# Memory tokens turned unscaled, two heads' key-query products ahead, and another order of the score products

## The chip, the cores and the metric

The kernel runs on one core of a Trainium2 chip. The metric is the device time of one execution in microseconds. TensorE (PE) multiplies matrices into PSUM, which has eight banks of 128 x 512 float32. VectorE (DVE) and ScalarE (ACT) work on data in SBUF and PSUM, and SyncE (SP) issues all the DMAs.

## The reference, cut to what matters

One decoder layer on x of 2048 x 1024, in float32, with 256 memory tokens: a recurrent and convolutional mixer, cross-attention into the memory, a gated feed-forward network and a last norm. The attention is the part that the change touches:

```python
h = rms_norm(x, xa_norm_g[l])
m = rms_norm(mem, mem_norm_g[l])                    # 256 x 1024
q = (h @ w_q[l]).reshape(bsz, s, XA_HEADS, XA_HD)   # 4 heads of 256
kv = m @ w_kv[l]
k, v = jnp.split(kv, 2, axis=-1)
...
scores = jnp.einsum("bshd,bmhd->bhsm", q, k).astype(jnp.float32) * (XA_HD ** -0.5)
p = jax.nn.softmax(scores, axis=-1).astype(v.dtype)
o = jnp.einsum("bhsm,bmhd->bshd", p, v).reshape(bsz, s, d)
x = x + o @ w_o[l]
```

Here rms_norm divides each token by the root of its mean square (plus 1e-6) and multiplies with a gain per channel.

## The kernel before

The kernel does not issue its instructions as it goes. Its Python code records operations (`Program.do`, `Program.dma`; all are issued from line 485), and a planner then simulates the engines at build time (`Program.schedule`, `Program.deadlines`) and writes out one fixed order for each engine. The order of the recorded matmuls gives each operation a due time; on each engine the ready operation with the earliest due time goes first. The durations that the planner assumes come from `estimate`. Operations recorded while `pr.first` is true come before all others. 28 passes are simulated, and the order of the shortest is written out. So a change of an assumed duration moves no work, but can move instructions within each engine's order, SP's DMAs included.

All large matmuls are done as three products of operands split into a high and a low part (`mm3`, names ending in h and l). ScalarE writes the high part and VectorE the low part.

The stages, in order of time:
- `memory_a` (start): the 256 memory tokens are loaded as four 128 x 512 tiles `mem`, squared and summed, scaled with their norm factor, transposed by TensorE with the identity, and copied with the channel gain to four tiles `mt` (channels x tokens). For each head, `kv` multiplies `mt` with columns of w_kv (`raw`) to give the keys, the columns of w_q are transposed (`qt`), and their product gives A, that is w_q times the keys: x times A is the scores. `HEADS` heads are done ahead of the first half's mixer, the other heads behind it (`mixed_in`).
- `mix_x`, `mix`: the tokens x are normed and transposed, and multiplied with w_in, in two halves of 1024 tokens. VectorE does the convolutions (`conv`) and the recurrence (`lru`, with one scan for each of 16 tiles), the second half's while the first half is in its attention.
- `attend(0)`, `attend(1)`: for each half of the tokens three matrix products (w_out, A, and VO, which is values times w_o), each done by `seven` as Strassen's scheme with seven block products P1 to P7. A product is 4 steps of inner blocks x 4 token blocks x 3 matmuls. It accumulates in a group of four PSUM banks, a or b; all eight are then taken. A product either starts a group afresh (True) or adds to what the group holds (False). When a product ends, the group is read into the blocks C11 to C22 that its row names; the next product on that group has to wait for these drains.
- For the second of the three (`SECOND`, the scores), the drains go to tiles `prob`: the first into a block is a copy by ScalarE, the later ones are additions by VectorE, and behind the last one the tile's softmax runs: maximum on VectorE, two exponentials with sums on ScalarE, a reciprocal, two scalings on ScalarE. Then `turn` transposes the block on TensorE to tiles `pt`, which the third product (`THIRD`) reads. The table given to `seven` says behind which product and which inner step a turn or a norm is recorded: (6, 0) is behind step 0 of the seventh product.
- `up`, `Down`, `finish`: the feed-forward network and the last norm, from about 1035 us to the end.

Of the kernel before, what the change touches and what calls it, by code (L numbers as in the profile page):

```python
# [62 lines left out]
STACKS = 2  # L63


def estimate(eng, name, n, pointer):
    if eng == "DVE":
        if name == "reciprocal":
            return 0.1 + n * 0.0063
        return (0.13 if name == "scalar_tensor_tensor" else 0.08) + n * 0.00104  # L70
    if eng == "Pool":
        return 0.18 + n * 0.0021
    return 0.1 + n * 0.00083 + 0.09 * pointer


class Buf:
# [90 lines left out]
class Program:  # L167
# [51 lines left out]
    def do(self, eng, name, out, *args, reads=(), writes=(), **kw):  # L219
        outs = [out] + ([kw["accum_out"]] if "accum_out" in kw else [])  # L220
        ins = [a for a in list(args) + list(kw.values()) if isinstance(a, Ref) and a not in outs]
        if eng == "PE":
            o = self.group or self.op("PE")
            n = ins[1].n if name == "matmul" else P
            if name == "matmul":
                cost = (n + 32) / 2400.0 if ins[1].rounded else n * 4 / 2400.0
            else:
                cost = 0.11
            self.clock += cost
            o.cost += cost  # L230
        else:
            o = self.op("Pool" if eng == "either" else eng)
            o.either = eng == "either"
            n = max(r.n for r in ins + outs)
            o.cost = estimate(o.eng, name, n, any(isinstance(a, Ref) for a in kw.values()))
            if eng == "DVE":
                self.vector = max(self.vector, self.clock) + o.cost
            if eng == "ACT":
                o.sets = ACT_SETS.get(args[1])
        o.calls.append((name, (out,) + args, kw))  # L240
        for r in outs:
            if not r.rounded:
                r.buf.loaded = False
        self.touch(
            o, [b for r in ins for b in r.parts()] + [b.parts[0] for b in reads],
            [b for r in outs for b in r.parts()] + [b.parts[0] for b in writes],
        )
# [72 lines left out]
    def schedule(self):  # L320
# [81 lines left out]
        def dispatch(e, t):  # L402
            if not idle[e]:
                return
            o = pick(e, t)
            if o is None:
                return
            idle[e] = False
            o.start, o.on = t, e
            order.append(o)  # L410
            if e == "PE":
                lag[0] += 0.2 * (t - o.turn - lag[0])
            cost = o.cost
            if e == "ACT" and o.sets is not None and table[0] not in o.sets:
                cost += ACT_SWITCH
                table[0] = o.sets[0]
            if o.either and e == "DVE":
                cost = estimate("DVE", "tensor_tensor", 1024, False)
            if e == "SP":
                dma_free[0] = max(dma_free[0], t) + cost  # L420
                push(max(t + 0.1, dma_free[0] - BACKLOG), 2, e)
                push(dma_free[0] + o.delay, 0, o)
            else:
                push(t + cost, 2, e)
                push(t + cost, 0, o)
# [87 lines left out]
def hybrid_layer(  # L513
# [25 lines left out]
    def ACT(out, in_, func, **k):  # L539
        pr.do("ACT", "activation", out, in_, func, **k)  # L540
# [14 lines left out]
    def ps():  # L555
        return pr.new("ps", name="ps")
# [57 lines left out]
    def small(w):  # L614
        at, n_small[0] = n_small[0], n_small[0] + w
        assert n_small[0] <= SMALLS, n_small
        return Buf(None, (P, w), smalls[:, at : at + w], F32, f"small{at}")
# [436 lines left out]
    VO_raw = Kept("VO1", 16, F32)  # L1054
    mt = []

    def kv(c0):
        t = tmp("kv")
        pp = [ps(), ps()]
        for kq in range(2):  # L1060
            st = raw_cols(w_kv[0], c0, kq)
            for f in range(2):
                with together():
                    for k in range(KQ):
                        sl = slice((k % 2) * M, (k % 2 + 1) * M)
                        matmul(pp[f][:, :M], st[:, k, f * P : (f + 1) * P], mt[kq * 2 + k // 2][:, sl], kq + k == 0, kq == 1 and k == KQ - 1)
            yield 0
        for f in range(2):
            ACT(t[:, f * M : (f + 1) * M], pp[f][:, :M], AF.Copy)
        return t  # L1070

    HEADS = 1

    def memory_a():
        pr.first = True
        xs = []
        for mb in range(2):
            parts = []
            ssp = small(2)
            for half in range(2):  # L1080
                t = tmp("mem")
                pr.dma(t[:], mem[0, mb * P : (mb + 1) * P, half * TT : (half + 1) * TT])
                square(t[:], ssp[:, half : half + 1], half == 1)
                parts.append(t)
            r = small(1)
            V("tensor_tensor", r[:], ssp[:, 0:1], ssp[:, 1:2], op=ALU.add)
            ACT(r[:], r[:], AF.Sqrt, bias=eps[:], scale=1.0 / D)
            V("reciprocal", r[:], r[:])
            for t in parts:
                ACT(t[:], t[:], AF.Copy, scale=r[:, 0:1])  # L1090
            xs.append(parts)
        for k2 in range(NK // 2):
            t = tmp("mt")
            p = ps()
            with together():
                for kk in range(2):
                    k = 2 * k2 + kk
                    for mb in range(2):
                        transpose(p[:, kk * M + mb * P : kk * M + (mb + 1) * P], xs[mb][k // 4][:, (k % 4) * P : (k % 4 + 1) * P], ident[:])
            for kk in range(2):  # L1100
                sl = slice(kk * M, (kk + 1) * M)
                ACT(t[:, sl], p[:, sl], AF.Copy, scale=vec["v1024"][:, 2 * k2 + kk, G_MEM : G_MEM + 1])
            mt.append(t)
        pr.first = False
        yield 2
        for h in range(4):
            if h == HEADS:
                yield mixed_in[0]
            kt = yield from kv(h * M)
            yield 0  # L1110

            qt = []
            for kq in range(2):
                st = raw_cols(w_q[0], h * M, kq)
                for db in range(2):
                    p = ps()
                    with together():
                        for j in range(KQ):
                            transpose(p[:, j * P : (j + 1) * P], st[:, j, db * P : (db + 1) * P], ident[:])
                    t = tmp("qt")  # L1120
                    ACT(t[:], p[:], AF.Copy)
                    qt.append(t)
            yield 1
            for k2 in range(NK // 2):
                p = ps()
                with together():
                    for kk in range(2):
                        k = 2 * k2 + kk
                        for db in range(2):
                            cs = slice((k % KQ) * P, (k % KQ + 1) * P)  # L1130
                            ks = slice(db * M, (db + 1) * M)
                            matmul(p[:, kk * M : (kk + 1) * M], qt[(k // KQ) * 2 + db][:, cs], kt[:, ks], db == 0, db == 1)
                r = tmp("a")
                ACT(r[:], p[:], AF.Copy)
                for kk in range(2):
                    k, cs, ks = 2 * k2 + kk, slice((h % 2) * M, (h % 2 + 1) * M), slice(kk * M, (kk + 1) * M)
                    i = k * 2 + h // 2
                    pr.dma(A_raw.at(i)[:, cs], r[:, ks], writes=[A_raw.tok.setdefault(i, Buf(None, (1,)))], join=True)
            yield 0
# [47 lines left out]
    class Blocks:  # L1187
# [5 lines left out]
        def get(self, key, i):  # L1193
            if key[0] == "A":
                return self.raw[int(key[1]) - 1, int(key[2]) - 1, i]
            if (key, i) not in self.s:
# [5 lines left out]
    PRODUCTS = dict(P1=("A11", "B11"), P2=("A12", "B21"), P3=("S4", "B22"), P4=("A22", "T4"), P5=("S1", "T1"), P6=("S2", "T2"), P7=("S3", "T3"))  # L1202
    FIRST = (("P1", "a", True, [C11]), ("P2", "b", True, [C11]), ("P6", "a", False, [C12]), ("P5", "b", True, [C22]),
             ("P7", "a", False, [C22]), ("P3", "b", False, [C12]), ("P4", "a", False, [C21]))
    SECOND = (("P1", "a", True, [C11]), ("P4", "b", True, [C21]), ("P2", "b", True, [C11]), ("P6", "a", False, [C12]), ("P5", "b", True, [C22]),
              ("P7", "a", False, [C21, C22]), ("P3", "b", False, [C12]))
    THIRD = (("P1", "a", True, [C11]), ("P4", "b", True, [C21]), ("P6", "a", False, [C12]), ("P5", "b", True, [C22]),
             ("P7", "a", False, [C21, C22]), ("P2", "a", True, [C11]), ("P3", "b", False, [C12]))

# [163 lines left out]
    def attend(h, ready):  # L1373
# [69 lines left out]
        def take_p(th, half, k, p):  # L1443
# [6 lines left out]
            (1, 3): pass_on(1).get(0, ()),  # L1450
            (3, 0): pass_on(1).get(1, ()),
            (6, 0): [lambda: turn(prob, 0, 0, take_p)],
        })
        del X
        st2 = [Stats(), Stats()]
# [9 lines left out]
        def norm_next(*steps):  # L1465
# [2 lines left out]
        yield fours[2]  # L1468
        yield from seven(THIRD, PT, VO_Q, add2, {
            (0, 1): [lambda: turn(prob, 1, 1, take_p)],  # L1470
            (0, 3): [lambda: turn(prob, 1, 0, take_p)],
            (0, 2): norm_next(0, 1, 2),
            (2, 0): norm_next(3),
            (2, 2): [lambda: turn(prob, 0, 1, take_p)],
# [445 lines left out]
```

## Time and profile before

| | |
|---|---|
| median of 3 runs | 2433.74 us (2433.09 to 2435.8) |
| the profiled execution, its own time | 2434.4 us |
| its span, first to last instruction | 2432.6 us |
| mean granted TensorE clock | 0.996 |
| PE busy | 2399.2 us (99%) |
| DVE busy | 1923.1 us (79%) |
| ACT busy | 1278.8 us (53%) |
| moved by DMA | 572.08 MB, mean 235 GB/s |

Busy is the time in which at least one instruction of the engine is under way. Matmuls overlap: a 128 x 512 one shows 390 ns, while the next one starts 0.23 us behind it, so a busy TensorE can still lose time when its clock is granted at less than full. A line of the timeline has the start in us, the busy time, engine, line of the code, operation, output<-input, and in brackets the idle time before it with what ended that. A line of the groups has the count, the busy time in us and the mean of one in ns. All recorded operations have one line, 485, so the names of the tiles tell them apart.

### The profile page before, as it was taken

The page shows a single profiled execution, that of the slowest core. Times are in us where ns is not written, and L with a number is a line of the kernel's source. Part 1 is how long each engine was busy: PE and PEld are TensorE (multiplying, and loading weights), DVE is VectorE, ACT ScalarE, POOL GpSimd, SP SyncE. Part 2 cuts the span into 40 slices and gives each one's busy share as a digit, 9 for nine tenths or more (in the row PEclk, how much of TensorE's full clock was granted, in tenths as well). Part 3 has the DMA queues.
Part 4 walks back from the last instruction along what each step waited for, and adds up shares of the span by engine and source line. Part 5 has one row for each costly group of instructions (what it writes and reads, how often), then busy time and mean ns, then how long its engine had stood idle before and what let it go on. Part 6 is the DMA issues. An engine that isn't in the chain of part 4 may idle for free.

```text
span 2432.6 us, 32495 instructions
## 1 busy us (share of the span) xinstructions
PE 2399.2 (99%) x10788; PEld 1979.2 (81%) x10788; DVE 1923.1 (79%) x3231; ACT 1278.8 (53%) x2246; POOL 0.7 (0%) x6
## 2 busy tenths in 40 slices
PE   7999999999999999999999999999999999999998
PEld 6888778888777888788888888888888888888887
DVE  5699979999999545897988878988787585667656
ACT  7438567467796457585554446555444331233222
POOL 0000000000000000000000000000000000000000
PEclk9999999999999999999999999999999999999999
DMA  8988898989787957556655446654442397789774
GB/s 285 322 312 278 268 312 278 299 267 313 263 283 259 327 188 260 173 183 229 234 199 190 165 161 215 234 183 156 160 143 70 104 314 259 249 277 355 230 240 169
DMA packets 344063, 572.08 MB, mean 235 GB/s; under 512 B 33052, under 2 KB 110876, under 8 KB 343894
## 3 DMA queue, kind: packets, MB, share of 16 engines
q1 hardware_dynamic: 343894, 570.00, 69.4%
q8 instruction: 85, 1.39, 0.2%
q14 instruction: 84, 0.69, 0.1%
HBM read 385.32 MB, written 184.55 MB: 234 GB/s over the span
## 4 chain that ended last, share of the span: by engine, by line
PE 71%; ACT 3%; DVE 1%; issue 0%; DMA 0%; DVEq 0%; ACTq 0%
PE ps L485 71%; ACT prob L485 2%; ACT yh L485 0%; ACT L485 0%; ACT pt L485 0%; DVE yl L485 0%; DVE acc L485 0%; DMA VO<-VO 0%; DVE smalls L485 0%; DMA VO<-yh 0%; DVE conv L485 0%; DVE gate L485 0%; DVE prob L485 0%; ACT m L485 0%; ACT sq L485 0%
## 5 line engine op out<-in xcount | busy, mean ns | idle before, releaser
L485 PE MATMUL ps<-Xh,wh 128*128 128x512 f32 x1344 | 523.6, 390 | 0.0
L485 PE MATMUL ps<-Xh,wl 128*128 128x512 f32 x1344 | 522.9, 389 | 0.0
L485 PEld LDWEIGHTS ps<-Xh,wl 128*128 128x128 f32 x1344 | 252.3, 188 | 52.5
L485 PEld LDWEIGHTS ps<-Xh,wh 128*128 128x128 f32 x1344 | 252.3, 188 | 52.2
L485 PE MATMUL ps<-wh,yh 128*128 128x512 f32 x672 | 266.7, 397 | 7.8 <-ACT prob L485 4.5
L485 PE MATMUL ps<-wl,yh 128*128 128x512 f32 x672 | 263.5, 392 | 0.1
L485 PE MATMUL ps<-wh,yl 128*128 128x512 f32 x672 | 263.5, 392 | 0.0
L485 PE MATMUL ps<-wl,hidh 128*128 128x512 f32 x672 | 261.4, 389 | 0.0
L485 PE MATMUL ps<-wh,hidh 128*128 128x512 f32 x672 | 261.4, 389 | 0.0
L485 DVE TENSOR_TENSOR acc<-acc,ps 128x512 f32<-128x512 f32 x192 | 129.4, 686 | 148.6 <-PE ps L485 147.8
L485 PE MATMUL ps<-wh,hidl 128*128 128x512 f32 x624 | 242.7, 389 | 0.0
L485 PE MATMUL ps<-Xl,wh 128*128 128x512 f32 x576 | 224.1, 389 | 0.0
L485 PE MATMUL ps<-xh,wh 128*128 128x512 f32 x512 | 203.9, 398 | 0.0
L485 PE MATMUL ps<-xh,wl 128*128 128x512 f32 x512 | 199.6, 390 | 0.3 <-DVE wl L485 0.3
L485 PE MATMUL ps<-xl,wh 128*128 128x512 f32 x512 | 199.5, 390 | 0.0
L485 ACT ACTIVATE wh<-s 128x512 fp32r<-128x512 f32 x192 | 119.5, 627 | 117.1 <-DVE s L485 57.3
L485 ACT ACTIVATE u<-ps 128x512 f32<-128x512 f32 x144 | 85.7, 595 | 150.1 <-PE ps L485 136.0
L485 PEld LDWEIGHTS ps<-wh,yh 128*128 128x128 f32 x672 | 127.5, 190 | 34.4 <-ACT prob L485 5.0
L485 DVE TENSOR_TENSOR wl<-s,wh 128x512 fp32r<-128x512 f32 x192 | 130.5, 688 | 28.2 <-PE ps L485 14.8
L485 PE MATMUL ps<-xn,wh 128*128 128x512 f32 x384 | 149.4, 389 | 0.0
L485 PE MATMUL ps<-tx,wh 128*128 128x512 f32 x384 | 149.4, 389 | 0.0
L485 PEld LDWEIGHTS ps<-wh,yl 128*128 128x128 f32 x672 | 127.2, 189 | 26.9 <-DVE yl L485 0.2
(209 smaller groups left out, 4513.1 us busy)
## 6 DMA issues: line engine op xcount, KB each, us to landing
raw<-in_w_up_dram SPq DMA_DIRECT2D x96, 512.0 KB
wh<-w_down SPq DMA_DIRECT2D x164, 256.0 KB
wl<-w_down SPq DMA_DIRECT2D x164, 256.0 KB
hid<-cv SPq DMA_DIRECT2D x48, 512.0 KB
h<-hid SPq DMA_DIRECT2D x96, 256.0 KB
w_down<-wh SPq DMA_DIRECT2D x84, 256.0 KB
x<-in_x_dram SPq DMA_DIRECT2D x64, 256.0 KB
wh<-w_out SPq DMA_DIRECT2D x56, 256.0 KB
```

The costliest lines, as they stand in the source:

```text
L485: getattr(e, name)(*[resolve(a) for a in args], **{k: resolve(a) for k, a in kw.items()})
```

## The change

- `memory_a` transposes the memory tiles as loaded. The squares, the norm factors r and what follows from them are recorded behind the transposes: the identity is scaled by r, a matmul with a matrix of 1/512 everywhere spreads it into a row on all partitions, and ScalarE copies that row twice, times 512, into the tile `rows`.
- The first head's keys are made from the unscaled `mt` and multiplied with `rows` by VectorE while they leave PSUM (before: a copy by ScalarE). Then the four tiles `mt` are multiplied with `rows` in place, for the other heads and the values.
- `HEADS` is 2: the second head's keys, transposes of w_q and products are recorded ahead of the first half's mixer.
- In `SECOND`, P7 comes ahead of P5.
- The turn of block (1, 0) is recorded in the scores' last product, (6, 2), instead of in the third product's first, (0, 3).
- `estimate` assumes other durations: reciprocal and scan on VectorE, and on ScalarE 0.09 us for each operand that is a pointer (before: 0.09 us for one or more).

```diff
@@ -63,14 +63,16 @@
 STACKS = 2
 
 
-def estimate(eng, name, n, pointer):
+def estimate(eng, name, n, pointers):
     if eng == "DVE":
         if name == "reciprocal":
-            return 0.1 + n * 0.0063
+            return 0.07 + n * 0.0063
+        if name == "tensor_tensor_scan":
+            return 0.13 + n * 0.00208
         return (0.13 if name == "scalar_tensor_tensor" else 0.08) + n * 0.00104
     if eng == "Pool":
         return 0.18 + n * 0.0021
-    return 0.1 + n * 0.00083 + 0.09 * pointer
+    return 0.1 + n * 0.00083 + 0.09 * pointers
 
 
 class Buf:
@@ -232,7 +234,7 @@
             o = self.op("Pool" if eng == "either" else eng)
             o.either = eng == "either"
             n = max(r.n for r in ins + outs)
-            o.cost = estimate(o.eng, name, n, any(isinstance(a, Ref) for a in kw.values()))
+            o.cost = estimate(o.eng, name, n, sum(isinstance(a, Ref) for a in kw.values()))
             if eng == "DVE":
                 self.vector = max(self.vector, self.clock) + o.cost
             if eng == "ACT":
@@ -415,7 +417,7 @@
                 cost += ACT_SWITCH
                 table[0] = o.sets[0]
             if o.either and e == "DVE":
-                cost = estimate("DVE", "tensor_tensor", 1024, False)
+                cost = estimate("DVE", "tensor_tensor", 1024, 0)
             if e == "SP":
                 dma_free[0] = max(dma_free[0], t) + cost
                 push(max(t + 0.1, dma_free[0] - BACKLOG), 2, e)
@@ -1054,7 +1056,7 @@
     VO_raw = Kept("VO1", 16, F32)
     mt = []
 
-    def kv(c0):
+    def kv(c0, rows=None):
         t = tmp("kv")
         pp = [ps(), ps()]
         for kq in range(2):
@@ -1066,10 +1068,13 @@
                         matmul(pp[f][:, :M], st[:, k, f * P : (f + 1) * P], mt[kq * 2 + k // 2][:, sl], kq + k == 0, kq == 1 and k == KQ - 1)
             yield 0
         for f in range(2):
-            ACT(t[:, f * M : (f + 1) * M], pp[f][:, :M], AF.Copy)
+            if rows is None:
+                ACT(t[:, f * M : (f + 1) * M], pp[f][:, :M], AF.Copy)
+            else:
+                V("tensor_tensor", t[:, f * M : (f + 1) * M], pp[f][:, :M], rows[:, f * M : (f + 1) * M], op=ALU.mult)
         return t
 
-    HEADS = 1
+    HEADS = 2
 
     def memory_a():
         pr.first = True
@@ -1080,14 +1085,7 @@
             for half in range(2):
                 t = tmp("mem")
                 pr.dma(t[:], mem[0, mb * P : (mb + 1) * P, half * TT : (half + 1) * TT])
-                square(t[:], ssp[:, half : half + 1], half == 1)
                 parts.append(t)
-            r = small(1)
-            V("tensor_tensor", r[:], ssp[:, 0:1], ssp[:, 1:2], op=ALU.add)
-            ACT(r[:], r[:], AF.Sqrt, bias=eps[:], scale=1.0 / D)
-            V("reciprocal", r[:], r[:])
-            for t in parts:
-                ACT(t[:], t[:], AF.Copy, scale=r[:, 0:1])
             xs.append(parts)
         for k2 in range(NK // 2):
             t = tmp("mt")
@@ -1101,12 +1099,27 @@
                 sl = slice(kk * M, (kk + 1) * M)
                 ACT(t[:, sl], p[:, sl], AF.Copy, scale=vec["v1024"][:, 2 * k2 + kk, G_MEM : G_MEM + 1])
             mt.append(t)
+        rows, p = tmp("rows"), ps()
+        for mb, parts in enumerate(xs):
+            ssp, r, t = small(2), small(1), tmp("diag")
+            for half in range(2):
+                square(parts[half][:], ssp[:, half : half + 1], half == 1)
+            V("tensor_tensor", r[:], ssp[:, 0:1], ssp[:, 1:2], op=ALU.add)
+            ACT(r[:], r[:], AF.Sqrt, bias=eps[:], scale=1.0 / D)
+            V("reciprocal", r[:], r[:])
+            ACT(t[:, :P], ident[:], AF.Copy, scale=r[:, 0:1])
+            matmul(p[:, mb * P : (mb + 1) * P], ones[:], t[:, :P], start=True, stop=True)
+        for i in range(2):
+            ACT(rows[:, i * M : (i + 1) * M], p[:, :M], AF.Copy, scale=float(DL))
         pr.first = False
         yield 2
         for h in range(4):
             if h == HEADS:
                 yield mixed_in[0]
-            kt = yield from kv(h * M)
+            kt = yield from kv(h * M, None if h else rows)
+            if not h:
+                for t in mt:
+                    V("tensor_tensor", t[:], t[:], rows[:], op=ALU.mult)
             yield 0
 
             qt = []
@@ -1202,8 +1215,8 @@
     PRODUCTS = dict(P1=("A11", "B11"), P2=("A12", "B21"), P3=("S4", "B22"), P4=("A22", "T4"), P5=("S1", "T1"), P6=("S2", "T2"), P7=("S3", "T3"))
     FIRST = (("P1", "a", True, [C11]), ("P2", "b", True, [C11]), ("P6", "a", False, [C12]), ("P5", "b", True, [C22]),
              ("P7", "a", False, [C22]), ("P3", "b", False, [C12]), ("P4", "a", False, [C21]))
-    SECOND = (("P1", "a", True, [C11]), ("P4", "b", True, [C21]), ("P2", "b", True, [C11]), ("P6", "a", False, [C12]), ("P5", "b", True, [C22]),
-              ("P7", "a", False, [C21, C22]), ("P3", "b", False, [C12]))
+    SECOND = (("P1", "a", True, [C11]), ("P4", "b", True, [C21]), ("P2", "b", True, [C11]), ("P6", "a", False, [C12]), ("P7", "a", False, [C21, C22]),
+              ("P5", "b", True, [C22]), ("P3", "b", False, [C12]))
     THIRD = (("P1", "a", True, [C11]), ("P4", "b", True, [C21]), ("P6", "a", False, [C12]), ("P5", "b", True, [C22]),
              ("P7", "a", False, [C21, C22]), ("P2", "a", True, [C11]), ("P3", "b", False, [C12]))
 
@@ -1450,6 +1463,7 @@
             (1, 3): pass_on(1).get(0, ()),
             (3, 0): pass_on(1).get(1, ()),
             (6, 0): [lambda: turn(prob, 0, 0, take_p)],
+            (6, 2): [lambda: turn(prob, 1, 0, take_p)],
         })
         del X
         st2 = [Stats(), Stats()]
@@ -1468,7 +1482,6 @@
         yield fours[2]
         yield from seven(THIRD, PT, VO_Q, add2, {
             (0, 1): [lambda: turn(prob, 1, 1, take_p)],
-            (0, 3): [lambda: turn(prob, 1, 0, take_p)],
             (0, 2): norm_next(0, 1, 2),
             (2, 0): norm_next(3),
             (2, 2): [lambda: turn(prob, 0, 1, take_p)],
```

## The prediction

> **What bounds the kernel now.** I read the page first, for the share of each engine and its clock, then the stages, then TensorE's waits, and last the chain of waits and the timeline around each wait.
>
> ```profile
> span 2432.6 us, 32495 instructions
> PE 2399.2 (99%) x10788; PEld 1979.2 (81%) x10788; DVE 1923.1 (79%) x3231; ACT 1278.8 (53%) x2246; POOL 0.7 (0%) x6
> ```
> ```profile
> 0.00:20.00 20.00, 9.36 (x43) 8.35 (x44) 9.00 (x35) 10.70 (x21) 0.70 (x6) 1.00 0.71 240
> 20.00:40.00 20.00, 18.30 (x105) 15.00 (x104) 12.70 (x43) 16.72 (x34) 0.00 (x0) 1.00 0.97 297
> 40.00:60.00 20.00, 19.96 (x104) 16.51 (x103) 12.57 (x62) 19.94 (x40) 0.00 (x0) 1.00 0.93 314
> 440.00:735.00 295.00, 284.76 (x1291) 232.99 (x1289) 291.63 (x506) 211.30 (x391) 0.00 (x0) 0.99 0.82 279
> 950.00:977.00 27.00, 24.11 (x128) 20.45 (x127) 18.81 (x48) 27.00 (x75) 0.00 (x0) 0.98 0.36 108
> 1200.00:2400.00 1200.00, 1200.00 (x5296) 993.66 (x5295) 910.98 (x1439) 491.31 (x793) 0.00 (x0) 1.00 0.61 207
> 2400.00:2433.00 33.00, 25.05 (x111) 20.42 (x109) 21.32 (x46) 10.44 (x32) 0.00 (x0) 0.96 0.35 128
> ```
> The second fence is the view by stages: length, then busy time of PE, PEld, DVE, ACT, POOL, then granted clock, DMA share, GB/s. TensorE is the bound: only 33.4 us of the span (2432.6 - 2399.2) are without a matmul. From 1200 to 2400 nothing is missing, so the up and down projections have nothing to give. Of the idle time 12.3 us lie in the first 40 us (10.64 + 1.70), 8 in the tail, which the change leaves alone, and 10.2 between 440 and 735, where VectorE is busy 291.6 of 295 us. The waits, in us, times, longest:
>
> ```profile
> PE ps L485 <- ACT mem L485: 7.2, 2, 6.5
> PE ps L485 <- ACT prob L485: 4.5, 1, 4.5
> PE ps L485 <- ACT pt L485: 3.4, 2, 2.9
> PE ps L485 <- ACT r L485: 2.8, 2, 2.1
> PE ps L485 <- DVE prob L485: 1.1, 2, 0.6
> ```
> All five are at places that the diff touches: memory tokens, score drains (prob), transposed probabilities (pt). A wait also costs what follows it:
>
> ```profile
> 638.63 0.80 PE L485 MATMUL ps<-wh,yh 128*128 128x512 f32 x1 [4.54 <-ACT prob L485]
> 641.66 0.40 PE L485 MATMUL ps<-wl,yh 128*128 128x512 f32 x1
> 725.76 1.04 PE L485 MATMUL ps<-ident,prob 128*128 128x128 f32 x8
> 735.63 0.80 PE L485 MATMUL ps<-wh,yh 128*128 128x512 f32 x1 [0.35 <-ACT yh L485]
> 737.07 0.40 PE L485 MATMUL ps<-wh,yh 128*128 128x512 f32 x1
> 971.88 1.91 PE L485 MATMUL ps<-ident,prob 128*128 128x128 f32 x16
> 976.67 0.80 PE L485 MATMUL ps<-wh,yh 128*128 128x512 f32 x1 [2.89 <-ACT pt L485]
> 982.82 0.40 PE L485 MATMUL ps<-wh,yl 128*128 128x512 f32 x1
> 976.67 1445.67 PE ps L485 x6404
> 717.21 8.22 ACT prob L485 x25
> 953.02 7.86 ACT prob L485 x24
> ```
>
> The last three rows are the chain of waits: from 976.67 on it is TensorE alone, at 1445.67 / 6404 = 0.226 us a matmul. Between the two attention halves it runs through ScalarE's softmax. With that pitch the loss at each place is:
> - 638: 4.54 us idle, then 7 matmuls in 3.03 us (638.63 to 641.66) instead of 1.58: 6.0 us.
> - 724 to 737: 32 transposes (8 at 725.76, 24 up to 735.63) and 4 matmuls take 737.07 - 725.76 = 11.3 us. At 1.91 / 16 = 0.12 us a transpose they need 4.7: 6.6 us.
> - 977: 2.89 us idle, then 14 matmuls in 6.15 us instead of 3.16: 5.9 us.
> - DVE prob (688): 1.1 us.
>
> Together 19.6 us, beside the idle time of the start.
>
> The slow matmuls behind a wait bear on a rule. The Trainium skill (TensorE: Matmul & The Clock Gate, "What's actually happening") says that the clock halves after an idle window of about 3.4 us and returns after about as long of work. The trace agrees on the half clock, but not on that length of wait: 2.89 us were enough, and the slow stretch behind it was 6.15 us. By the rule the 977 wait would cost an estimated 2.89 + 1.7 = 4.6 us and the sum below would be 1.3 us smaller; the measured row decides.
>
> **The change part by part. Start.** Rows of the timeline before:
>
> ```profile
> 4.74 0.43 SPq L485 DMA_DIRECT2D raw<-in_w_kv_dram  x1
> 6.91 0.63 ACT L485 ACTIVATE junk<-mem 128x512 f32<-128x512 f32 x1 [0.69 <-DMA mem<-in_mem_dram]
> 8.42 0.69 DVE L485 SCALAR_TENSOR_TENSOR junk<-mem 128x512 f32<-128x512 f32 x1 [1.29 <-DMA mem<-in_mem_dram]
> 10.88 0.48 PE L485 MATMUL ps<-ident,mem 128*128 128x128 f32 x1 [6.47 <-ACT mem L485]
> 12.10 3.46 PE L485 MATMUL ps<-ident,mem 128*128 128x128 f32 x15 [0.74 <-ACT mem L485]
> 15.36 7.81 PE L485 MATMUL ps<-mt,raw 128*128 128x256 f32 x32
> 16.89 0.69 DVE L485 SCALAR_TENSOR_TENSOR junk<-x 128x512 f32<-128x512 f32 x1 [1.49 <-DMA x<-in_x_dram]
> 33.74 1.15 ACT L485 ACTIVATE wh<-raw 128x512 fp32r<-128x512 f32 x2 [1.72 <-DMA raw<-in_w_in_dram]
> ```
> ```profile
> L485 ACT ACTIVATE mem<-mem,smalls 128x512 f32<-128x512 f32 x4 | 2.6, 710 | 0.4 <-DVE smalls L485 0.4
> L485 ACT ACTIVATE prob<-ps 128x512 f32<-128x512 f32 x32 | 18.3, 592 | 1.2 <-DVE gate L485 0.4
> L485 DVE TENSOR_TENSOR prob<-prob,ps 128x512 f32<-128x512 f32 x32 | 20.0, 681 | 9.9 <-PE ps L485 9.9
> L485 DVE TENSOR_TENSOR_SCAN gate<-xc,hlast,gate 128x512 f32<-128x512 f32 x16 | 20.5, 1284 | 0.1
> L485 ACT ACTIVATE prob<-prob,smalls 128x256 f32<-128x256 f32 x128 | 64.7, 553 | 0.8 <-DVE smalls L485 0.7
> L485 ACT ACTIVATION_READ_ACCUMULATOR prob<-prob,smalls 128x1 f32 x64 | 12.6, 197 | 0.0
> ```
> Unscaled, the transposes need no square, root, reciprocal or scaling (four of 710 ns go). The first eight wait for the third tile, landed by 6.91, the others for the fourth, by 8.42. Sixteen take 0.48 + 3.46 = 3.9 us, so they end near 11.0 instead of 15.36: 4.3 us. The 32 matmuls of the key projection then need w_kv, whose landing the trace doesn't show, because nobody waited for it. Bounds: landed already (4.3 us won), or landed at 15.36 (nothing). In between, after the last memory tile come two x tiles and the first w_kv load, 1.05 MB, at 240 to 297 GB/s 3.5 to 4.4 us: about 12.5; the second half is issued ahead of the x tile that was awaited until 16.89. So its 16 matmuls (half of 7.81) end near 16.9 + 3.9 = 20.8 instead of 23.2. I take -2.5 us, the nearest to rows, with ends 0 and -4.5.
>
> New work: two 128-wide matmuls for the row (0.13 us each by 1.04 / 8), TensorE +0.3 us. Two scalings of the identity and two row copies on ScalarE, each at most 710 ns, under 3 us; on VectorE two products off the banks, half of 681 ns each, and four products on mt, 681 each: 3.4 us. Cover: VectorE is idle for 7.3 us between 20 and 40 and 7.4 between 40 and 60. The first head's copies leave ScalarE, behind which the scaling of x stood. The four products on mt are waited for by the second head's key matmuls alone.
>
> Second head early: 32 matmuls (7.8 us), 16 transposes (1.9), 16 matmuls of the same 128x256 shape (3.9): 13.6 us of TensorE work that are only moved, so nothing by themselves. They are filler, because dense work begins when w_in lands (33.74). But SP gets 4 loads of 512 KB and 8 stores of 128 KB ahead of w_in, 12 issues of 0.43 = 5.2 us, and at 297 GB/s 2.1 MB of loads are 7.1 us. w_in slides to about 41, and the filler ends near 34.4 - 2.5 + 13.6 = 45.5. It holds, so I cost this at 0; without that cover it would be up to +7.
>
> **Score order.** P7 ahead of P5 completes block (1,0) one product earlier (48 matmuls, 10.8 us), and its turn moves into the last score product. A tile's softmax costs ScalarE (64.7 + 12.6) / 32 = 2.4 us. In the second half the two blocks came together, eight tiles, while ScalarE had stood idle just before:
>
> ```profile
> 949.92 0.60 ACT L485 ACTIVATE pt<-ps 128x512 f32<-128x512 f32 x1 [13.44 <-PE ps L485]
> ```
> and then was busy 27.00 of 27 us. Four tiles, 9.7 us, fit the idle 13.44, more than the 2.89 that was missing. I take -5.9 us (ends -5.9 and -1).
>
> In the first half the same move helps, but VectorE is full from 440 to 735 and little in that stretch can be put off: the convolutions of the second half must end before its attention. A wait removed there can come back as a wait for VectorE. Of 6.0 + 6.6 + 1.1 = 13.7 us I take a little under half, -6 (ends 0 and -13.7).
>
> **New seams.** P6 and P7 use bank group a back to back, and P5 and P3 bank group b. Before, another product lay between. The next product may overwrite a bank once its drain is done: 592 ns (copy) or 681 ns (add), while TensorE still has the other three banks, 9 x 0.226 = 2.0 us. With a free engine nothing is lost; behind a softmax or a table load it is up to the 6.0 us of the wait at 638, which is such a drain. Four seams: I take 0.5 us each, +2 (ends 0 and +24).
>
> **Estimates.** They alter no instruction, only the order written out. The scan was planned at 0.08 + 512 x 0.00104 = 0.61 us and takes 1.284; the new figure is 1.19, so 16 scans put the plan back by 9 us less. That is part of my -6 and has no term of its own. Past 1200 TensorE misses nothing that a new order could give back; it could lose there, unlikely with VectorE at 76%.
>
> Sum: -2.5 + 0.3 + 0 - 5.9 - 6 + 2 = -12.1 us. The profiled execution took 2434.4 us (1.8 beside the span), the median of the runs is 2433.7. So 2434.4 - 12.1 = 2422.3, and against the median 2421.6: I say 2422.
>
> **The rivals.**
> - VectorE bound: what is won before 735 comes back as waits for VectorE. For it: 98.9% busy there. Against it: VectorE is idle for 25.7 us in the first 60 us, which work moved ahead could use. Left are -5.9 and some of the start: about 2428.
> - All waits go: -19.6 and -4.3 at the start: 2410. For it: all are ScalarE queue effects; against it, again VectorE.
> - Seams decide: four late drains of 6.0 us cost 24 and leave +10: about 2444, slower. It decides from 3.5 us a seam (14.1 won in all but the seams). For it: ScalarE held such a drain for 4.54 us at 638; against it: in the second half ScalarE idled.
> - The change does not do what it says: the new order doesn't start memory work earlier, because w_kv is late and the moved loads push w_in; then the start is 0 to +7 and the total 2424 to 2431.
>
> **How the numbers follow.** Chances: my case 0.48 (own range 2415 to 2427), VectorE 0.17, all gone 0.15, seams 0.1, start fails 0.1. The range for 8 in 10 goes from 2411 to 2432. From no change a measurement here tells about 0.2%, 4.9 us, so faster means under 2428.9. That holds my case, the all-gone one, and half of the VectorE and start cases, less a little for an order gone wrong: 0.76 faster, 0.14 same, 0.10 slower.
>
> **What would show it.** Start: memory transposes before 9 us, no "ACT mem" wait, less than 10 us idle in the first 40. Second half: no wait for pt near 970, ScalarE busy in two blocks there. First half: the wait at 638 under 2 us, VectorE still full. Seams: waits of the first P7 or P3 matmul for ACT or DVE prob. Wrong would be me if TensorE waits sum to over 30 us outside the tail, or if any waits appear after 1200.

## The result, and the profile after

The changed kernel takes 2416.27 us (median of 5 runs, 2416.18 to 2418.29), the kernel before 2433.74. The ratio is 0.993, with a 95% interval from 0.9919 to 0.9942. The forecast was 2422 in a range from 2411 to 2432. The page of the changed kernel, and then TensorE's waits in it (us in total, times, longest):

```profile
span 2414.1 us, 32342 instructions
PE 2392.8 (99%) x10792; PEld 1974.7 (82%) x10792; DVE 1926.8 (80%) x3237; ACT 1273.1 (53%) x2242; POOL 0.7 (0%) x6
```
```profile
PE ps L487 <- DMA mem<-in_mem_dram: 3.9, 2, 3.5
PE ps L487 <- DMA raw<-in_ffn_norm_g_dram: 3.3, 1, 3.3
PE ps L487 <- DVE xl L487: 1.3, 1, 1.3
PE ps L487 <- ACT yh L487: 1.3, 2, 1.0
...
PE ps L487 <- ACT prob L487: 0.6, 2, 0.3
```
The span is 18.5 us shorter. TensorE without a matmul went from 33.4 to 21.3 us: 12.1 us. Its busy time fell by 6.4 us although it does four matmuls more; I put those 6.4 down to matmuls that no longer run slowly behind a wait. ScalarE's `mem`, `pt` and `r` are gone from the list; memory tokens are now waited for as loads.

Where the 12.1 us came from shows in TensorE's busy time up to four points of the timeline, first of the kernel before, then of the changed one (stage, its length, PE busy with count, granted clock, DMA share, GB/s):

```profile
0.00:60.00 60.00, 47.62 (x248) 1.00 0.87 284
0.00:600.00 600.00, 586.82 (x2664) 1.00 0.87 293
0.00:740.00 740.00, 717.02 (x3252) 0.99 0.85 286
0.00:1000.00 1000.00, 974.13 (x4468) 0.99 0.82 278
```
```profile
0.00:60.00 60.00, 51.04 (x281) 1.00 0.86 286
0.00:600.00 600.00, 591.04 (x2701) 1.00 0.87 294
0.00:740.00 740.00, 726.30 (x3311) 1.00 0.86 290
0.00:1000.00 1000.00, 986.30 (x4556) 1.00 0.83 281
```
The lead is 3.4 us at 60, 4.2 at 600, 9.3 at 740 and 12.2 at 1000, and stays there. With the slow matmuls, the start is worth 3.4 us, the second half's attention 2.9 + 3.0 = 5.9, and the first half's some 9.3 (5.9 of waits between 60 and 740, and the other 3.4 of the 6.4 us, which is what is left over and not measured row by row). That makes 18.6.

The start of the changed kernel:

```profile
4.66 0.48 PE L487 MATMUL ps<-ident,mem 128*128 128x128 f32 x1 [0.38 <-DMA mem<-in_mem_dram]
8.63 3.46 PE L487 MATMUL ps<-ident,mem 128*128 128x128 f32 x15 [3.49 <-DMA mem<-in_mem_dram]
11.88 3.86 PE L487 MATMUL ps<-mt,raw 128*128 128x256 f32 x16
17.75 1.89 PE L487 MATMUL ps<-mt,raw 128*128 128x256 f32 x8
25.99 1.06 PE L487 MATMUL ps<-ident,raw 128*128 128x128 f32 x8 [0.88 <-DMA raw<-in_w_q_dram]
43.54 0.47 PE L487 MATMUL ps<-xh,wh 128*128 128x512 f32 x1
```
The transposes go as the tiles land and end near 12 instead of 15.4; the first head's keys are done at 19.6 instead of 23.2. The dense mixer work begins at 43.5 (before: 34.4), with the second head's work in between. The second half's attention, by stages (PE, PEld, DVE, ACT, POOL busy), first before, up to the point where ScalarE became busy, then the changed kernel, up to that point and behind it:

```profile
936.00:950.00 14.00, 14.00 (x67) 11.65 (x66) 5.28 (x9) 0.56 (x2) 0.00 (x0) 1.00 1.01 360
```
```profile
936.00:950.00 14.00, 14.00 (x80) 12.07 (x79) 6.83 (x19) 12.45 (x33) 0.00 (x0) 1.00 0.39 114
950.00:977.00 27.00, 27.00 (x129) 22.61 (x128) 24.39 (x48) 20.88 (x50) 0.00 (x0) 1.00 0.54 164
```
ScalarE now does four tiles' softmax in the 14 us in which it had stood idle (0.56 us busy, now 12.45), and in the 27 us behind them it is no longer full. In the first half waits are left. The two longest come first, then what is left of the wait at 638 (P2 behind P4's drain, 4.54 us before), then the one at the new seam, within P7:

```profile
629.04 0.50 PE L487 MATMUL ps<-xl,gwah 128*128 128x512 f32 x1 [1.26 <-DVE xl L487]
654.81 0.50 PE L487 MATMUL ps<-wh,yh 128*128 128x512 f32 x1 [1.01 <-ACT yh L487]
631.48 0.50 PE L487 MATMUL ps<-wh,yh 128*128 128x512 f32 x1 [0.31 <-ACT prob L487]
659.25 0.50 PE L487 MATMUL ps<-wh,yh 128*128 128x512 f32 x1 [0.25 <-ACT prob L487]
440.00:735.00 295.00, 290.26 (x1318) 235.87 (x1317) 290.71 (x507) 218.43 (x400) 0.00 (x0) 1.00 0.84 283
```
The last row is the stage as a whole. The granted clock is 1.00 there (0.99 before), so none of these waits lost the clock, and VectorE is as full as before: 290.71 us of 295.

### The profile page after: what moved, and what is told of

It is laid out like the page before. It is cut to its first block, busy times and chain, and to the rows that moved or that the text cites. A ratio compares the mean times of both kernels' runs of the same rounds, so it can differ in the third digit from the quotient of the medians.

```text
span 2414.1 us, 32342 instructions
## 1 busy us (share of the span) xinstructions
PE 2392.8 (99%) x10792; PEld 1974.7 (82%) x10792; DVE 1926.8 (80%) x3237; ACT 1273.1 (53%) x2242; POOL 0.7 (0%) x6
## 4 chain that ended last, share of the span: by engine, by line
PE 72%; DVE 1%; ACT 0%; DMA 0%; issue 0%; DVEq 0%; SPq 0%; ACTq 0%
PE ps L487 72%; DVE acc L487 0%; ACT L487 0%; DVE yl L487 0%; DMA VO<-VO 0%; DMA wl<-A 0%; DVE gate L487 0%; DVE s L487 0%; DVE xc L487 0%; DVE f L487 0%; ACT gate L487 0%; DVE conv L487 0%; DVE so L487 0%; ACT m L487 0%; ACT yh L487 0%
```

## The experiments

All times are medians in us, ratios to the kernel before timed beside it, with 95% intervals.

**The parts alone.** The score order alone:

```diff
-    SECOND = (... ("P6", "a", False, [C12]), ("P5", "b", True, [C22]), ("P7", "a", False, [C21, C22]), ...
+    SECOND = (... ("P6", "a", False, [C12]), ("P7", "a", False, [C21, C22]), ("P5", "b", True, [C22]), ...
+            (6, 2): [lambda: turn(prob, 1, 0, take_p)],
...
-            (0, 3): [lambda: turn(prob, 1, 0, take_p)],
```


> The kernel before with the score order and the moved turn alone (P7 ahead of P5, block (1,0) turned in the scores' last product). Theory (softmax queue on ScalarE is what both attention halves wait for): the wait near 977 goes with the slow matmuls behind it (-5.9 us) and the 724 to 737 stretch loses most of its 6.6 us; the wait near 638 stays, since it is the drain of P4 and lies ahead of the moved products: 2421 to 2424 us, about -10 to -12. Rival (VectorE bound in the first half): only the second half's 5.9 us go, 2427 to 2429, and what goes at 724 comes back as waits for VectorE.

Measured: 2425.15, ratio 0.9966 (0.9954 to 0.9979). Its stages and its longest wait:

```profile
936.00:950.00 14.00, 14.00 (x72) 11.83 (x71) 7.55 (x23) 11.28 (x31) 0.00 (x0) 1.00 0.62 220
950.00:977.00 27.00, 27.00 (x137) 22.81 (x136) 19.29 (x43) 23.64 (x63) 0.00 (x0) 1.00 0.43 135
```
```profile
661.98 0.50 PE L485 MATMUL ps<-wh,yh 128*128 128x512 f32 x1 [2.73 <-ACT prob L485]
```
The second half behaves as in the changed kernel: this part gives its 5.9 us without help of the others. The first half has new waits at other places, 2.73 us of them at 661.98, where the drain of one score product (ScalarE's copy to `prob`) holds TensorE. The clock went soon behind it, too (the row of 661.98 still shows 0.50 us, but the granted clock from 662.5 to 666 is 0.51). The total, 8.7 us, lies between the two theories.

The new assumed durations alone:

```diff
-            return 0.1 + n * 0.0063
+            return 0.07 + n * 0.0063
+        if name == "tensor_tensor_scan":
+            return 0.13 + n * 0.00208
...
-    return 0.1 + n * 0.00083 + 0.09 * pointer
+    return 0.1 + n * 0.00083 + 0.09 * pointers
```


> The kernel before with the new assumed durations alone: same instructions, another order. Theory: the planner knows the scan's 1.28 us, so the drain at 638 is no longer late: that wait and its slow matmuls go (-6.0), the waits at 724 and 977 stay: about 2428 us. Rival: the plan's figures matter no more than any other shuffling of the order: 2432 to 2437, some waits moved elsewhere.

Measured: 2427.64, ratio 0.9973 (0.9964 to 0.9982). The sum is as forecast, its parts are not. The wait of 4.54 us at 638 is replaced by shorter ones of 1.9 and 1.7 us, but the first half also has this one:

```profile
730.21 0.79 PE L487 MATMUL ps<-wh,yh 128*128 128x512 f32 x1 [5.11 <-ACT yh L487]
```
And the second half's wait for `pt`, which was to stay, is down to 0.7 us, in the old score order.

The start alone (tokens unscaled, row of factors, two heads ahead):

```diff
-                square(t[:], ssp[:, half : half + 1], half == 1)
...
-                ACT(t[:], t[:], AF.Copy, scale=r[:, 0:1])
...
+        rows, p = tmp("rows"), ps()
+            matmul(p[:, mb * P : (mb + 1) * P], ones[:], t[:, :P], start=True, stop=True)
...
-    HEADS = 1
+    HEADS = 2
```


> The kernel before with the start alone: tokens turned unscaled, row of norm factors, two heads ahead. Theory: TensorE is ahead by the 3.4 us that the changed kernel shows at 60 us, and keeps them to the end because only a wait that VectorE sets could swallow them: about 2430.5 us. Rival (VectorE is full from 380 on and its last work for the second half sets the pace): the 3.4 us are swallowed by longer waits between 600 and 740, 2433 to 2435.

Measured: 2432.77, ratio 0.9996 (0.9987 to 1.0005): no gain that can be told. At 60 us the lead is there, 51.38 - 47.62 = 3.8 us:

```profile
0.00:60.00 60.00, 51.38 (x282) 1.00 0.86 287
```
In the profiled execution, 2430.9 us and the lowest of 11, it stays to the end: the theory's figure. The median lost some 2 us of it again; the interval reaches from -3.2 to +1.2 us and tells the two theories not apart.

**The order itself as a control.** The kernel before with one assumed time changed that belongs to no part:

```diff
-HOP = 0.3
+HOP = 0.31
```


> A control: the kernel before with the planner's assumed time from engine to engine 0.31 us instead of 0.30, nothing else. It shows how much any other order written out moves the time. Theory (the effects of the change have causes of their own): within 2 us of 2433.7. Rival (the order is luck): off by 4 us or more, either way.

Measured: 2437.35, ratio 1.0019 (1.001 to 1.0028), 3.5 us slower. In the first half it has this wait, which the kernel before does not have:

```profile
734.81 1.12 PE L485 MATMUL ps<-ident,prob 128*128 128x128 f32 x4 [9.24 <-ACT prob L485]
```
The same tweak on the changed kernel:

> The second control: the changed kernel with the planner's assumed time from engine to engine 0.31 us instead of 0.30. Theory (ScalarE and VectorE have room in the new order): within 2 us of 2416.3. Rival (as in the first control, which lost 3.5 us between 660 and 760): 2418 to 2421 us, with the second half free of waits in any case.

Measured: 2423.93, ratio 0.9961 (0.9948 to 0.9973), 7.7 us slower than the changed kernel. Its second half is free of waits, its start keeps the lead (50.7 us busy of the first 60). What it lost lies in the first half, the longest of it here:

```profile
707.70 4.19 PE L487 MATMUL ps<-ident,prob 128*128 128x128 f32 x16 [2.84 <-ACT prob L487]
```
So a new order written out can move the first half by some microseconds, as it did both times, and differences of this size between two kernels can't be put down to the part that was changed, unless its own place in the trace shows it.

**The parts undone.** The score order and turn put back:

> The changed kernel with the score order and the turn put back. Theory (the parts add up; the order alone was worth 8.7 us): 2416.3 + 8.7 = 2425 us, with the wait for pt of the second half back. Rival (the new durations give the plan room enough; with them alone the second half waited 0.7 us for pt instead of 2.9): 2418 to 2421 us.

Measured: 2424.85, ratio 0.9961 (0.9949 to 0.9974). The total is that of the first theory and the cause is not: the wait did not come back.

```profile
950.00:977.00 27.00, 27.00 (x137) 22.85 (x136) 21.11 (x48) 26.73 (x71) 0.00 (x0) 1.00 0.43 133
727.14 0.79 PE L487 MATMUL ps<-wh,yh 128*128 128x512 f32 x1 [4.96 <-ACT yh L487]
```
ScalarE is still full there (26.73 of 27), but TensorE misses nothing. The loss is in the first half, 4.96 us of it at 727.

The old durations put back:

> The changed kernel with the old assumed durations. Theory (the parts add up; the durations alone were worth 6.3 us): 2422 to 2423 us, all of the loss in waits between 600 and 760, none in the second half. Rival (the durations only shuffle): 2415 to 2419 us.

Measured: 2418.32, ratio 0.9936 (0.9923 to 0.9948): 2.1 us, the rival's figure. The first half has waits of 3.8 us in all between 600 and 760, the second none.

One head ahead instead of two:

> The changed kernel with one head ahead instead of two. Theory (the second head fills TensorE until w_in lands): without it TensorE has nothing to do for some microseconds between 20 and 40, so most of the 3.4 us won at the start are lost: 2418 to 2420 us. Rival (the second head's loads push w_in back as much as it fills): the same, 2415 to 2417 us, and the lead at 60 us unchanged.

Measured: 2434.2, ratio 1.0001 (0.9992 to 1.001). All is lost, far outside both theories. TensorE waits 4.01 us for w_q here, and behind that its clock is low:

```profile
26.71 1.09 PE L487 MATMUL ps<-ident,raw 128*128 128x128 f32 x4 [4.01 <-DMA raw<-in_w_q_dram]
26.00:33.00 7.00, 6.29 (x31) 6.32 (x32) 2.47 (x13) 4.82 (x10) 0.00 (x0) 0.52 1.14 330
0.00:60.00 60.00, 49.41 (x257) 0.94 0.89 290
PE ps L487 <- DVE yl L487: 8.1, 3, 5.8
```
Slow matmuls count as busy, so the 49.41 us at 60 flatter this kernel: 6.29 us at a clock of 0.52 are, by an estimate, 3.0 us less work. That leaves 49.41 - 3.0 = 46.4, behind the kernel before (47.62). So the whole lead of the start is gone, as the first theory has it and more. The rest goes in the first half, with waits for VectorE longer than in any other of these kernels (last row, between 600 and 660: us, times, longest).

**What the first half waits for.** Here the order written out stays the same on every engine, and only durations are cut; on ScalarE the table loads that are no longer needed go (17 in the kernel before, 21 in the changed one).

```diff
             ACT(t[:], p[:], AF.Sigmoid, bias=w[:, bi : bi + 1])
+            instead(q, AF.Tanh)        # emitted in place of the sigmoid for q >= 2
...
         ACT(m[:], m[:], AF.Sqrt, scale=-1.0)
+        instead(q, AF.Copy)
```


> The kernel before in its own order, with ScalarE's table loads taken out of the second half's recurrences alone: at eight tiles the sigmoids are emitted as tanh and the square root as a copy, so that its output is another. The planner still reckons with the old functions, so the order on TensorE, VectorE and SyncE is the same; 17 table loads go, 17 x 1.28 = 22 us of ScalarE. Theory A (ScalarE's queue sets the waits between 600 and 740): the wait at 638 goes and the later ones shrink: 2424 to 2428 us. Theory B (VectorE sets them): 2431 to 2434 us. The wait of 2.9 us near 977 stays in both.

Measured: 2431.61, ratio 0.9993 (0.9985 to 1.0002). The wait of 4.54 us at 638 became three, each ended by a copy on ScalarE (second fence), and each of those behind something that waited for VectorE:

```profile
635.60 0.50 PE L485 MATMUL ps<-wh,yh 128*128 128x512 f32 x1 [1.70 <-ACT prob L485]
638.79 0.50 PE L485 MATMUL ps<-wh,yh 128*128 128x512 f32 x1 [0.83 <-ACT prob L485]
641.98 0.50 PE L485 MATMUL ps<-wh,yh 128*128 128x512 f32 x1 [1.53 <-ACT prob L485]
```
```profile
634.44 0.63 ACT L485 ACTIVATE m<-m 128x512 f32<-128x512 f32 x1 [1.62 <-DVE m L485]
638.14 0.60 ACT L485 ACTIVATE prob<-ps 128x512 f32<-128x512 f32 x1 [1.58 <-DVE s L485]
641.33 0.60 ACT L485 ACTIVATE prob<-ps 128x512 f32<-128x512 f32 x1 [1.55 <-DVE gate L485]
```
That is 4.06 us in place of 4.54. ScalarE, relieved, has time there, but the places in its order are fixed.

```diff
             V("scalar_tensor_tensor", ev, every(back - 2 * i, m), tap(2 * i), ev, op0=ALU.mult, op1=ALU.add)
+            narrow(h)                  # emitted on the first 384 columns for the second half
```


> The kernel before in its own order, with VectorE relieved by about the same amount: the 176 tap operations of the second half's convolution are emitted 384 instead of 512 columns wide (the last quarter of them is left out of the result), about 176 x 0.13 = 23 us. Theory A (ScalarE's queue): 2430 to 2434 us. Theory B (VectorE is the bound from 440 to 735): the waits between 600 and 740 go, 2420 to 2425 us. The wait near 977 stays in both.

Measured: 2432.47, ratio 0.9993 (0.9984 to 1.0002). VectorE is no longer full over the stage, and the wait is the same to the hundredth:

```profile
440.00:735.00 295.00, 285.36 (x1294) 234.21 (x1293) 278.21 (x507) 211.84 (x392) 0.00 (x0) 0.98 0.83 279
638.16 0.79 PE L485 MATMUL ps<-wh,yh 128*128 128x512 f32 x1 [4.54 <-ACT prob L485]
```
The stretch ahead of that drain in the kernel before shows why neither cut alone helps:

```profile
628.47:638.00 9.53, 5.62 (x25) 4.32 (x23) 9.53 (x15) 9.41 (x11) 0.00 (x0) 1.00 0.62 216
L485 ACT ACT_TABLE_LOAD x4 | 5.1, 1283 | 0.1
```
VectorE (9.53 us) and ScalarE (9.41 us, 5.1 of them four table loads) are both full there.

The same two cuts in the changed kernel:

> The changed kernel in its own order, with the same table loads taken out. 4.7 us of waits are left between 622 and 648. Theory A: most of them go, 2412 to 2414 us. Theory B: 2415 to 2416.5 us.

> The changed kernel in its own order, with the same taps narrowed. Theory A: 2415 to 2416.5 us. Theory B: the waits between 622 and 648 go, 2411 to 2413 us.

Measured: 2415.52 and 2417.03, against 2416.27, so less than 1 us either way. Between 600 and 760 TensorE is without a matmul for 5.0 and 4.8 us (160 - 154.99, 160 - 155.20), against 4.7 in the changed kernel (160 - 155.26). Neither ScalarE's time alone nor VectorE's alone sets what the first half loses: in the kernel before, each cut came out as the theory of the other engine has it. What fits is the order: a drain stands in ScalarE's queue behind an operation that itself waits for VectorE, or behind table loads, and the next matmul behind the drain. Cut one, and the other ends last. Both cuts at once were not tried, so this stays an explanation that agrees with the waits shown, and why the changed kernel's order loses less is not shown.

## Why the prediction was right, and where not

The time, 2416.3, lies in the range, and nearly all of the likeliest case's signs hold (no wait for `mem` on ScalarE, none for `pt` near 970, 0.31 us left of the wait at 638; the memory transposes end near 12, not 11). But its terms were not all of the right size: their sum, -12.1 us, is 5.4 short of the measured -17.5 (2416.27 - 2433.74).

- Start, -2.5 + 0.3: 3.4 us of lead at 60 us. The mis-sized term is the landing of w_kv. The second half of the keys was put at 20.8 us, because its load was thought to come behind the x tiles; in the changed order both w_kv loads go ahead of x, and the keys end at 19.6. What came late next was w_q, with 0.9 us, and here the profile is a lucky one: the six other kernels with two heads ahead waited 1.5 to 3.2 us for w_q, two of them with the very same order (1.9 and 2.5). The row of norm factors took four short matmuls and not two, 0.46 us instead of 0.3 (15.57 to 15.80 and 17.52 to 17.75 us). That the second head holds until w_in is there came true: dense work starts at 43.5, forecast 45.5, with no idle time between 40 and 60.
- The second half, -5.9: exactly that, 2.89 us of wait and 3.0 of slow matmuls. The four tiles fit the idle ScalarE as reckoned. The 3.0 hang on the clock, though: the same wait of 2.89 us was followed by anything from no slow matmuls to 6.15 us of them (last section), so this term is 2.9 to 5.9 us. What the prediction did not see is that the new durations alone let the planner find another way around this wait.
- The first half, -6: it lost 9.3 us less. The step that failed is its reason, that VectorE at 98.9% sets the pace and gives back what is won. In the changed kernel VectorE is still busy 290.7 of 295 us, and 9.3 us went all the same; with 13 us less on VectorE (278.2 of 295 instead of 291.6) the waits stayed as they were. Half of the reason holds: with ScalarE alone relieved, 4.06 of the 4.54 us came back behind VectorE. How much the first half loses hangs on the order that comes out: the controls put it 3.5 and 7.7 us elsewhere.
- The new seams, +2: 0.25 us at P7 (659.25) in the changed kernel and nothing at P3. The mechanism is real, though: with the score order alone the seam at P7 cost 2.73 us.
- The estimates, inside the -6 and without a term of their own: alone they give 6.3 us and undone they cost 2.1. The first control moved the time by 3.5 with no change of substance, so no size can be told for them.
- The parts do not add up. Alone they give 8.7, 6.3 and 1.1 us, undone they cost 8.6, 2.1 and (one head instead of two) 17.9. What stays with its part is the absence of the second half's wait in all seven kernels with the new score order, and, less surely, a lead at the start: with two heads ahead TensorE is busy 2.3 to 3.8 us longer than before in the first 60 us. That is an upper figure, since in four of these seven kernels the granted clock there is only 0.94 to 0.97; in the one with 0.94 (the changed kernel with table loads taken out) little of the lead can be left. These two can be called the change's own. Of the first half's 9.3 us, up to 7.7 may be the luck of the order that came out: the second control, with every part in place, lost as much.

## What to carry to other kernels

Where a planner writes out the order, shift one of its constants by a hair and time that too, before a gain of a few microseconds is credited to an edit: here it moved the time by 3.5 and 7.7 us. Look for the gain at its own place in the trace, where an engine stood idle and then was full; moving a block's last product ahead into ScalarE's 13 idle microseconds worked in every kernel that had it. An engine at 99% is not the bound until cutting its work moves the waits.

## What the runs showed of the hardware

A wait of 2.89 us at the same place, ended by the same ScalarE copy, had three outcomes. One kernel each:

```profile
975.10 0.50 PE L485 MATMUL ps<-wh,yh 128*128 128x512 f32 x1 [2.89 <-ACT pt L485]
973.98 0.50 PE L485 MATMUL ps<-wh,yh 128*128 128x512 f32 x1 [2.89 <-ACT pt L485]
974.57 0.63 PE L485 MATMUL ps<-wh,yl 128*128 128x512 f32 x1
980.70 0.79 PE L485 MATMUL ps<-wh,yh 128*128 128x512 f32 x1 [2.89 <-ACT pt L485]
```
The first (the kernel before with table loads taken out) kept the clock: the granted clock from 975 to 983 is 1.00. The second (the start alone, two rows) goes on at 0.50 us and loses the clock only behind the wait: from 974.5 to 978 it is 0.51. The third (the first control) starts slowly at once, with 0.79 us, as do the narrowed taps and the kernel before, which stayed slow for 6.15 us. So the duration of the first matmul behind a wait does not tell whether the clock was kept; the granted clock does. A shorter wait was enough elsewhere, in the kernel with the new durations alone, where the granted clock from 635.4 to 639.2 is 0.56:

```profile
635.46 0.50 PE L487 MATMUL ps<-xh,gwah 128*128 128x512 f32 x1 [1.94 <-ACT prob L487]
636.17 0.63 PE L487 MATMUL ps<-xh,gwal 128*128 128x512 f32 x1
```
The Trainium skill (TensorE: Matmul & The Clock Gate, "What's actually happening") puts the loss of the clock at an idle window of about 3.4 us that runs freely. That it runs freely agrees with one wait having three outcomes; that a wait has to be as long as the window does not, since 1.94 us were enough. This also fits the spread: the kernel before took from 2431.1 to 2436.9 us in 27 runs, the changed one, with no wait over 1.3 us behind the first 10 us of its profile, from 2416.2 to 2418.3 in 5.
